# A two-layer RWKV-7 / GLA trunk on one core: `solve` takes its heads in turn, and the inversions, loads and scores of later blocks are placed earlier among the weight products

## The chip, the core and the metric

The kernel runs on one core of a Trainium2 chip. The metric is the device time in microseconds (us) of one execution, as the median over several runs. The engines: PE multiplies matrices (its weight loads are shown apart as PEld), DVE and ACT work on vectors, POOL here only fills memory, SP issues DMAs. Each engine takes its instructions in order.

## The reference

16 learned tokens are put ahead of 256, which makes T = 272 tokens of 2048 numbers. Two layers follow, each a token mixer and a squared-ReLU MLP (2048 to 8192 and back), with RMS norms before each and residual additions. The mixer of layer 1 is gated linear attention. The mixer of layer 0, where the change lies, is RWKV-7: 32 heads of 64, and for each head a 64x64 state that every token updates:

```python
sa = einsum('bhvk,bhk->bhv', S, a_t)
S = S * w_t[:, :, None, :] + sa[..., None] * b_t[:, :, None, :] + v_t[..., None] * k_t[:, :, None, :]
y = einsum('bhvk,bhk->bhv', S, r_t)
...
y = ((y - mu) * rsqrt(var + GN_EPS)) * ln_w + ln_b
out = ((y + bonus) * g) @ w_o
```

All is float32.

## The kernel before

**Weight products.** Activations lie with features on partitions and tokens along the free axis. A float32 product with a weight is made of three matmuls: each weight tile of 128x1024 is loaded (`raw`, L129), split by ACT into `hi` (L135) and by DVE into the rest `lo` (L136), and multiplied as hi by x, hi by the rest of x, lo by x (L141 to L143). `raw` has three buffers, `hi` and `lo` two each. Eight such triples use up one tile. I call a triple a unit; in the stage below `R(n)` writes n units, and `until(m)` as many as bring their number to m.

**The recurrence.** It runs in chunks of tokens, four of 64 and one of 16 (c = 0 to 4), for 16 heads at a time (g = 0, 1). A block is a pair of chunks of one g: block 0 holds chunks 0 and 1, block 1 chunks 2 to 4, blocks 2 and 3 the same for g = 1. For a block, `load(b)` fetches the keys and queries, written to memory before, into the tiles BK and AR (L419; two sets of tiles, for even and for odd blocks). `scores(c, e)` multiplies them for eight heads (L436, two PSUM banks `pt`), and DVE masks the result into AM (L269, "mask" below). `invert(b)` inverts the 64x64 triangles of all heads at once on DVE: transposes into `sysA` (L450, L455), 30 pairs of operations `upd`, `sysA` ("steps"), transposes back (L466 into a place that the merge reads, L470 into AM). It is a generator, and `some(inv, n)` emits n pieces of it. `merge(b)` (L557, L567, on PE) joins the halves of the triangles.

Per chunk, on PE: `state` (L629, L631: what the state S contributes), `solve` (L641: the inverse times the right side `rs`), `centre` (L580, of the next chunk), `carry` (L648: S itself), `learn` (L654: the new state in PSUM, which DVE scales into `sb`, shown as S), `inner` (L603, of the next chunk), `emit` (L663: the outputs), `keys` (L593: keys of the next chunk, transposed). `sides`, `centre`, `solve`, `emit` and `keys` are evicted by ACT. `uv` holds the values of the chunk in one half of the partitions and what `solve` gives in the other.

When a g is through, `norm(g)` takes four features' tiles at a time: a matmul (L681), two ACT operations, three of DVE (L687, L269, L693) and four matmuls with the gate (L692); `split` makes of the result the operands of the output product.

**What sets the order.** On PE the order is written out by hand in this stage (`manual_schedule`): the chunk steps, with units between them that cover their latencies. GAPS gives for each chunk the units before `solve` and after `carry`; MARK gives the number of units at which each of the four merges stands. For all other engines a scheduler chooses the order when the kernel is built; then it is fixed, and waits follow from it.

```python
                for h in range(q, 16, 2):
                    nc.tensor.matmul(pu[o : o + nu, h // 2], am[up, h, :nu], rs[up, h], start=True, stop=True)
                nc.scalar.copy(uv[n : n + nu, q::2], pu[o : o + nu])
```

Of the kernel before, what the change touches and what calls it, by code (L numbers as in the profile page):

```python
# [43 lines left out]

GAPS = [[(4, 4), (4, 4), (5, 4), (5, 4), (5, 5)],
        [(4, 4), (4, 4), (5, 4), (5, 4), (5, 5)]]

MARK = [120, 176, 244, 326]  # L50

OUTQ = [0, 1, 4, 5]
OUTA = [4, 5, 6, 7, 12, 13, 14, 15]
# [2 lines left out]
class Kern:  # L56
# [210 lines left out]
    def rwkv(self, done):  # L267
        nc, tc, ap = self.nc, self.tc, self.ap
# [329 lines left out]
        def inner(g, c):  # L598
            full, n, nr, am, lo, up, at = geom(c)
            uv = uvs[g, c]  # L600
            ra = ras[g, c] = bank(self.pu())
            for h in range(16):
                nc.tensor.matmul(ra[at[h % 2], h // 2], am[:n, h, :n], uv[:n, h], start=h < 2, stop=c == 0 and h > 13)  # L603
            if c == 0:
                sides(g, c)
# [28 lines left out]
        def solve(g, c):  # L634
            full, n, nr, am, lo, up, at = geom(c)
            uv, rs, pu = uvs[g, c], ras[g, c, "rs"], bank(self.pu())
            nu = n if full else 16
            for q in range(2):
                o = n * (1 - q)
                for h in range(q, 16, 2):  # L640
                    nc.tensor.matmul(pu[o : o + nu, h // 2], am[up, h, :nu], rs[up, h], start=True, stop=True)  # L641
                nc.scalar.copy(uv[n : n + nu, q::2], pu[o : o + nu])


# [22 lines left out]
        def norm(g):  # L667

            def square(f):
                sq = self.t(kp, [P, T], "ysq", 2)  # L670
                nc.scalar.activation(sq, hres[:, f], AF.Square)
                return sq

            nxt = square(4 * g)
            yield
            for f in range(4 * g, 4 * g + 4):
                sq = nxt
                g2 = self.t(kp, [P, 2, P], "g2", 2)
                nc.sync.dma_start(g2, ap["g2"][f])
                va = self.pry()[:, :T]  # L680
                nc.tensor.matmul(va, self.bones, sq, start=True, stop=True)  # L681
                nc.scalar.activation(sq, va, AF.Ln, scale=1.0 / HEAD, bias=self.eps[GN_EPS])
                nc.scalar.activation(sq, sq, AF.Exp, scale=-0.5)
                if f < 4 * g + 3:
                    nxt = square(f + 1)
                yield
                nc.vector.scalar_tensor_tensor(out=sq, in0=hres[:, f], scalar=self.vec("ln_w", f), in1=sq, op0=ALU.mult,  # L687
                                               op1=ALU.mult)
                tt(rr[f], rr[f], sq, ALU.add)
                pg = self.pm()[:, :T]  # L690
                for i in range(2):
                    nc.tensor.matmul(pg, g2[:, i], gs[i], start=i == 0, stop=i == 1)  # L692
                nc.vector.scalar_tensor_tensor(out=hres[:, f], in0=rr[f], scalar=self.vec("ln_b", f), in1=pg,  # L693
                                               op0=ALU.add, op1=ALU.mult)
                normed.add(f)
                yield
# [82 lines left out]
        def R(n):  # L779
            for _ in range(n):  # L780
                if next(work, work) is not work:
                    ran[0] += 1
# [4 lines left out]
        def some(it, n):  # L787
            for _ in range(n):
                next(it, None)

        nothing = iter(())
        self.split_parts = 2
        load(1)
        ahead()
        with tc.manual_schedule(engines={mybir.EngineType.PE}):
            R(10)
            for c, e in ((2, 0), (2, 1), (3, 0), (3, 1), (4, 0)):
                some(inv, 7)
                R(16)
                scores(c, e)  # L800
            for g in range(2):
                last, quarter = nothing, 0
                if g:

                    last = norm(0)
                    some(last, 1)
                    for _ in range(4):
                        R(3)
                        some(last, 2)
                    last = chain(last, norm(1))  # L810
                until(MARK[2 * g])
                some(inv, 99)
                m = merge(2 * g)
                next(m)
                some(last, 1)
                R(4)
                some(last, 1)
                next(m)
                some(last, 1)
                until(128 + 128 * g)  # L820
                centre(g, 0)
                some(last, 1)
                R(2)
                keys(g, 0)
                some(last, 1)
                R(2)
                inner(g, 0)
                some(last, 3)
                if g:

                    for c, e in ((2, 0), (2, 1), (3, 0), (3, 1), (4, 0)):
                        R(3)
                        scores(c, e)
                        some(last, 2)
                    assert next(last, None) is None
                else:
                    R(2)
                inv = invert(2 * g + 1)
                for c in range(5):
                    if c == 2:  # L840
                        until(MARK[2 * g + 1])
                        some(inv, 99)
                        m = merge(2 * g + 1)
                        next(m)
                        R(4)
                        next(m)
                        R(4)
                    if c:
                        state(g, c)
                    if g == 0 and c in (2, 3):  # L850
                        scores(c - 2, 0)
                    R(GAPS[g][c][0])
                    some(inv, 11)
                    solve(g, c)
                    if c < 4:
                        centre(g, c + 1)
                    if g == 0 and c in (2, 3):
                        scores(c - 2, 1)
                    if c < 4:
                        carry(g, c)  # L860
                    R(GAPS[g][c][1])
                    if g == 0 and c == 3:
                        inv = invert(2)
                    some(inv, 11)

                    if c < 4:
                        learn(g, c)
                        inner(g, c + 1)
                    emit(g, c)
                    if c < 3:  # L870
                        keys(g, c + 1)
                    if g == 0 and c == 1:
                        load(2)
                    if g == 0 and c == 4:
                        load(3)
            for g in (2, 3):
                for _ in norm(g):
                    R(g)
# [256 lines left out]
```

## Time and profile before

| | |
|---|---|
| median of three runs | 2623.42 us (2621.15 to 2627.11) |
| the profiled execution | 2624.24 us |
| its span, first to last instruction | 2622.0 us |
| PE busy | 2555.0 us, 97% |
| DVE busy | 1667.9 us, 64% |
| ACT busy | 1239.7 us, 47% |
| mean granted clock of PE | 0.987 |

The profile is of one execution. A row of a group reads: line, engine, operation, out<-in, size, count, then busy time and mean of one in ns, then the idle time of the engine just before such instructions and what ended it. A float32 matmul shows as two instructions, so eight heads are x16. In a table of stretches each row gives the stretch, its length, the busy time of PE, PEld, DVE, ACT and POOL with their counts, the clock that PE was granted (1.00 is full) and the share and rate of the DMA engines. A list of waits gives the waiting engine and line, who released it, the sum in us, how often, and the longest.

### The profile page before, as it was taken

What the parts mean: (1) busy time and instruction counts of PE and PEld (TensorE: products, weight loads), DVE (VectorE), ACT (ScalarE), POOL (GpSimd) and SP (SyncE); (2) the same over time, 40 slices, a digit from 0 to 9 for tenths busy, and PEclk for the clock granted to TensorE, in tenths of its full rate; (3) what the DMA queues carried; (4) which work ended last, traced back from release to release, by engine and by line L of the source; (5) the groups of instructions that cost most, each with busy time, mean ns of one, the idle gap of its engine ahead of it and who ended that gap; (6) DMA issues with size and microseconds to landing.
All of it is one profiled execution on the core that took longest, in us unless ns stands there. A gap on an engine that the chain in (4) does not pass through costs nothing.

```text
span 2622.0 us, 47088 instructions
## 1 busy us (share of the span) xinstructions
PE 2555.0 (97%) x19274; PEld 2364.8 (90%) x19274; DVE 1667.9 (64%) x2745; ACT 1239.7 (47%) x1941; POOL 9.3 (0%) x32
## 2 busy tenths in 40 slices
PE   9999799889999999999999999999999999999998
PEld 8898788788999999999999989998888888888887
DVE  8687985774755545545546676677766666656665
ACT  5376343434544434434434454455555535445344
POOL 0000000000000000000000000000000000000000
PEclk9999899889999999999999999999999999999999
DMA  5578543312455555555555544454555555555554
GB/s 201 175 239 276 195 138 98 115 67 86 164 175 176 177 177 177 177 176 175 175 176 176 178 151 149 145 173 153 185 189 189 187 191 186 190 188 187 191 185 160
DMA packets 140120, 450.13 MB, mean 172 GB/s; under 512 B 14704, under 2 KB 30832, under 8 KB 139904
## 3 DMA queue, kind: packets, MB, share of 16 engines
q1 hardware_dynamic: 139904, 447.12, 50.4%
q8 instruction: 151, 2.47, 0.4%
q14 instruction: 65, 0.53, 0.1%
HBM read 431.07 MB, written 15.99 MB: 171 GB/s over the span
## 4 chain that ended last, share of the span: by engine, by line
PE 78%; DVE 2%; ACT 1%; DMA 0%; issue 0%; DVEq 0%
PE pj L169 24%; PE pj L141 13%; PE pj L143 13%; PE pj L142 13%; PE pj L170 12%; DVE lo L136 1%; PE pt L970 1%; PE pu L641 0%; PE pu L979 0%; PE pm L692 0%; PE pt L959 0%; PE pu L981 0%; PE pry L681 0%; PE pm L580 0%; PE pm L916 0%; PE pu L980 0%
## 5 line engine op out<-in xcount | busy, mean ns | idle before, releaser
L135 ACT CAST hi<-raw 128x1024 fp32r<-128x1024 f32 (+2 forms) x838 | 814.0, 979 | 1121.4 <-PE pj L142 612.7
L136 DVE TENSOR_TENSOR lo<-raw,hi 128x1024 fp32r<-128x1024 f32 (+2 forms) x838 | 946.7, 1136 | 601.4 <-ACT hi L135 593.4
L141 PE MATMUL pj<-x,hi 128*128 128x272 f32 x2272 | 676.7, 298 | 6.1 <-DVE hres L269 4.1
L143 PE MATMUL pj<-x,lo 128*128 128x272 f32 x2272 | 661.0, 291 | 1.7 <-DVE lo L136 1.7
L142 PE MATMUL pj<-x,hi 128*128 128x272 f32 x2272 | 659.3, 290 | 0.0
L169 PE MATMUL pj<-x,hi 128*128 128x512 f32 x1664 | 585.8, 396 | 0.6 <-DVE x L889 0.6
L170 PE MATMUL pj<-x,lo 128*128 128x256 f32 x1664 | 466.7, 281 | 1.3 <-DVE lo L136 1.3
L141 PEld LDWEIGHTS pj<-x,hi 128*128 128x128 f32 x2272 | 431.9, 190 | 16.9 <-issue 6.1
L142 PEld LDWEIGHTS pj<-x,hi 128*128 128x128 f32 x2272 | 434.6, 191 | 4.2 <-issue 2.0
L143 PEld LDWEIGHTS pj<-x,lo 128*128 128x128 f32 x2272 | 431.6, 190 | 2.9 <-DVE lo L136 1.9
L169 PEld LDWEIGHTS pj<-x,hi 128*128 128x128 f32 x1664 | 312.5, 188 | 76.7 <-issue 2.9
L169 PE MATMUL pj<-h,hi 128*128 128x512 f32 x1024 | 358.5, 394 | 0.0
L170 PEld LDWEIGHTS pj<-x,lo 128*128 128x128 f32 x1664 | 313.3, 188 | 2.2 <-DVE lo L136 1.9
L141 PE MATMUL pj<-h,hi 128*128 128x272 f32 x1024 | 294.7, 288 | 0.0
L143 PE MATMUL pj<-h,lo 128*128 128x272 f32 x1024 | 293.9, 287 | 0.0
L142 PE MATMUL pj<-h,hi 128*128 128x272 f32 x1024 | 293.6, 287 | 0.0
L170 PE MATMUL pj<-h,lo 128*128 128x256 f32 x1024 | 288.5, 282 | 0.0
L169 PEld LDWEIGHTS pj<-h,hi 128*128 128x128 f32 x1024 | 192.4, 188 | 44.5
L142 PEld LDWEIGHTS pj<-h,hi 128*128 128x128 f32 x1024 | 193.7, 189 | 0.0
L170 PEld LDWEIGHTS pj<-h,lo 128*128 128x128 f32 x1024 | 193.5, 189 | 0.0
L141 PEld LDWEIGHTS pj<-h,hi 128*128 128x128 f32 x1024 | 192.6, 188 | 0.0
L143 PEld LDWEIGHTS pj<-h,lo 128*128 128x128 f32 x1024 | 192.1, 188 | 0.0
(247 smaller groups left out, 2095.4 us busy)
## 6 DMA issues: line engine op xcount, KB each, us to landing
raw<-mlp_w_d SPq DMA_DIRECT2D x512, 512.0 KB, 3.3
raw<-gla_in_d SPq DMA_DIRECT2D x98, 512.0 KB, 3.3
raw<-w_rkv_d SPq DMA_DIRECT2D x80, 512.0 KB, 3.5
raw<-gla_o_d SPq DMA_DIRECT2D x32, 512.0 KB, 3.3
raw<-rw_oQ_d SPq DMA_DIRECT2D x24, 512.0 KB, 3.3
raw<-w_r_d SPq DMA_DIRECT2D x16, 512.0 KB, 3.3
ard<-ar SPq DMA_DIRECT2D x16, 288.0 KB, 3.6
bkd<-bk SPq DMA_DIRECT2D x16, 288.0 KB, 4.0
```

What stands on the lines that cost most here:

```text
L135: nc.scalar.copy(hi[:, h], raw[:, h])
L136: nc.vector.tensor_tensor(out=lo[:, h], in0=raw[:, h], in1=hi[:, h].bitcast(F32), op=ALU.subtract)
L141: nc.tensor.matmul(out, hi[:, ws], xh, start=first, stop=False)
L142: nc.tensor.matmul(out, hi[:, ws], xl, start=False, stop=False)
L143: nc.tensor.matmul(out, lo[:, ws], xh, start=False, stop=last)
L169: nc.tensor.matmul(wide, hi[:, ws], x[kt][:, :, off : off + SEQ], start=kt == 0, stop=False)
L170: nc.tensor.matmul(ps[:, :SEQ], lo[:, ws], x[kt][:, 0, off : off + SEQ], start=False, stop=kt == nk - 1)
L970: nc.tensor.matmul(pa[:w, i * C : (i + 1) * C], KX[i][:, dt, s * P : s * P + w], Q[:, dt, i * C : (i + 1) * C], start=dt == 0, stop=dt == 1)
```

## The change

Nothing is computed in another way. `solve` issues its 16 heads in their order, which alternates between the two halves of the output's partitions, and both evictions come after the last. GAPS are smaller, and are the same for both g: 2 or 3 units after `carry` instead of 4, 4 before `solve` instead of 5 in chunks 2 and 3. Merges 1, 2 and 3 stand at fewer units. 26 units instead of 10 are written ahead of the first loop over block 1's scores, each of whose blocks has 16 more before it. For g = 1 the scores of block 3 move from behind merge 2 to between the pieces of `norm(0)`, and all of `norm(1)` behind merge 2. `invert(2g + 1)` is begun right behind merge 2g and spread over what follows; `invert(2)` begins one step sooner, as `scores(1,1)` does. The loads of blocks 2 and 3 are split in two, the keys first.

```diff
-GAPS = [[(4, 4), (4, 4), (5, 4), (5, 4), (5, 5)],
-        [(4, 4), (4, 4), (5, 4), (5, 4), (5, 5)]]
-MARK = [120, 176, 244, 326]
+GAPS = [(4, 2), (4, 2), (4, 2), (4, 3), (5, 5)]
+MARK = [120, 170, 240, 310]
...
+            for h in range(16):
+                o = n * (1 - h % 2)
+                nc.tensor.matmul(pu[o : o + nu, h // 2], am[up, h, :nu], rs[up, h], start=True, stop=True)
             for q in range(2):
                 o = n * (1 - q)
-                for h in range(q, 16, 2):
-                    nc.tensor.matmul(pu[o : o + nu, h // 2], am[up, h, :nu], rs[up, h], start=True, stop=True)
                 nc.scalar.copy(uv[n : n + nu, q::2], pu[o : o + nu])
...
+        units1 = ((2, 0), (2, 1), (3, 0), (3, 1), (4, 0))
...
-            R(10)
-            for c, e in ((2, 0), (2, 1), (3, 0), (3, 1), (4, 0)):
+            R(26)
+            for c, e in units1:
                 some(inv, 7)
                 R(16)
                 scores(c, e)
             for g in range(2):
-                last, quarter = nothing, 0
+                last = nothing
                 if g:
                     last = norm(0)
                     some(last, 1)
-                    for _ in range(4):
+                    for c, e in units1:
                         R(3)
                         some(last, 2)
-                    last = chain(last, norm(1))
+                        scores(c, e)
+                    last = norm(1)
                 until(MARK[2 * g])
                 some(inv, 99)
                 m = merge(2 * g)
                 next(m)
                 some(last, 1)
                 R(4)
-                some(last, 1)
                 next(m)
-                some(last, 1)
+                inv = invert(2 * g + 1)
+                some(inv, 4)
                 until(128 + 128 * g)
...
-                some(last, 3)
-                if g:
-                    for c, e in ((2, 0), (2, 1), (3, 0), (3, 1), (4, 0)):
-                        R(3)
-                        scores(c, e)
-                        some(last, 2)
-                    assert next(last, None) is None
-                else:
+                for _ in last:
                     R(2)
-                inv = invert(2 * g + 1)
+                    some(inv, 2)
+                R(2)
                 for c in range(5):
...
                     if g == 0 and c in (2, 3):
-                        scores(c - 2, 0)
-                    R(GAPS[g][c][0])
-                    some(inv, 11)
+                        scores(c - 2, c - 2)
+                        if c == 3:
+                            inv = invert(2)
+                    R(GAPS[c][0])
+                    some(inv, 9)
                     solve(g, c)
                     if c < 4:
                         centre(g, c + 1)
-                    if g == 0 and c in (2, 3):
-                        scores(c - 2, 1)
+                    if g == 0 and c == 2:
+                        scores(0, 1)
                     if c < 4:
                         carry(g, c)
-                    R(GAPS[g][c][1])
-                    if g == 0 and c == 3:
-                        inv = invert(2)
-                    some(inv, 11)
+                    R(GAPS[c][1])
+                    some(inv, 9)
                     if c < 4:
                         learn(g, c)
                         inner(g, c + 1)
+                    if g == 0 and c == 2:
+                        scores(1, 0)
                     emit(g, c)
                     if c < 3:
                         keys(g, c + 1)
-                    if g == 0 and c == 1:
-                        load(2)
-                    if g == 0 and c == 4:
-                        load(3)
+                    if g == 0:
+                        if c == 0:
+                            fetch(2, BKs, bkd)
+                        if c == 1:
+                            fetch(2, ARs, ard)
+                        if c == 2:
+                            fetch(3, BKs, bkd)
+                        if c == 4:
+                            fetch(3, ARs, ard)
+                    some(inv, 7)
```

How this moves instructions on engines whose order the scheduler makes. SP, at the load of block 1, before (`raw` are weights; BK and AR the block's tiles; `g` the gate's weights) and, in the second list, after:

```order
L129 DMA raw_3716<-w_rkv_d 128x1024
L419 DMA BK_618_3436<-bkd_79 128x8x320
L129 DMA raw_3751<-w_rkv_d 128x1024
L419 DMA AR_619_3437<-ard_80 128x8x320
L679 DMA g_877_5521<-g_d 128x256
```

```order
L128 DMA raw_3683<-w_rkv_d 128x1024
L418 DMA BK_618_3436<-bkd_79 128x8x320
L128 DMA raw_3718<-w_rkv_d 128x1024
L128 DMA raw_3783<-w_rkv_d 128x1024
L418 DMA AR_619_3437<-ard_80 128x8x320
L128 DMA raw_3818<-w_rkv_d 128x1024
```

One more weight stands between BK and AR.

DVE in `norm(0)`, between S of chunk 3 and the end of inversion 2, before and after (`upd` and `sysA` are steps of the inversion, `AM<-pt` masks of block 3):

```order
L687 SCALAR_TENSOR_TENSOR ysq_5510<-hres_72,vecs_121,ysq_5510 128x272
L269 TENSOR_TENSOR sysA_1934<-sysA_1934,upd_5410 64x17x14
L269 TENSOR_TENSOR r_7_81<-r_7_81,ysq_5510 128x272
L136 TENSOR_TENSOR lo_5564<-raw_5561,hi_5563 128x512 x2
L269 TENSOR_TENSOR upd_5458<-sysA_1934 64x240
L693 SCALAR_TENSOR_TENSOR hres_72<-r_7_81,vecs_121,pm_5531 128x272
L269 TENSOR_TENSOR sysA_1934<-sysA_1934,upd_5458 64x16x15
L687 SCALAR_TENSOR_TENSOR ysq_5527<-hres_72,vecs_121,ysq_5527 128x272
```

```order
L687 SCALAR_TENSOR_TENSOR ysq_5485<-hres_72,vecs_121,ysq_5485 128x272
L268 TENSOR_TENSOR upd_5317<-sysA_1934 64x238
L268 TENSOR_TENSOR r_7_81<-r_7_81,ysq_5485 128x272
L268 TENSOR_TENSOR sysA_1934<-sysA_1934,upd_5317 64x14x17
L693 SCALAR_TENSOR_TENSOR hres_72<-r_7_81,vecs_121,pm_5514 128x272
L268 TENSOR_TENSOR upd_5382<-sysA_1934 64x234
L268 TENSOR_TENSOR AM_620_3438<-pt_5518,cst_120 128x4x128
L268 TENSOR_TENSOR sysA_1934<-sysA_1934,upd_5382 64x13x18
L268 TENSOR_TENSOR AM_620_3438<-pt_5519,cst_120 128x4x128
L268 TENSOR_TENSOR upd_5385<-sysA_1934 64x228
L687 SCALAR_TENSOR_TENSOR ysq_5510<-hres_72,vecs_121,ysq_5510 128x272
```

Two masks now stand between one tile's norm and the next. From S of chunk 3 to the last transpose of inversion 2 DVE's queue holds, before, 60 steps, 6 transposes back, 5 `lo`, 4 norms, 7 additions and 4 transposes into the merge's place; after, 48 steps, the same transposes, 5 `lo`, 4 norms, 10 masks, 2 additions and 4 first transposes of inversion 3. From there to S of chunk 0 of g = 1 it holds, after, 44 steps of inversion 3, 12 transposes, 7 `lo`, 4 norms, 8 splits and 9 additions.

DVE again, around that S of g = 1, before and after. In `upd` the last number is the row's size; the steps begin with 30 and grow to 240 and shrink again:

```order
L269 TENSOR_TENSOR upd_6210<-sysA_1934 128x108
L269 TENSOR_TENSOR r_8_82<-pj_6088,r_8_82 128x272
L269 TENSOR_TENSOR sysA_1934<-sysA_1934,upd_6210 128x27x4
L136 TENSOR_TENSOR lo_6341<-raw_6338,hi_6340 128x512 x2
L269 TENSOR_TENSOR upd_6213<-sysA_1934 128x130
L269 TENSOR_TENSOR sysA_1934<-sysA_1934,upd_6213 128x26x5
L269 TENSOR_TENSOR S_3440<-pu_6187,WC_97 128x512
```

```order
L268 TENSOR_TENSOR upd_6249<-sysA_1934 128x210
L268 TENSOR_TENSOR sysA_1934<-sysA_1934,upd_6249 128x10x21
L268 TENSOR_TENSOR r_8_82<-pj_6138,r_8_82 128x272
L268 TENSOR_TENSOR upd_6252<-sysA_1934 128x198
L135 TENSOR_TENSOR lo_6396<-raw_6393,hi_6395 128x512 x2
L268 TENSOR_TENSOR sysA_1934<-sysA_1934,upd_6252 128x9x22
L268 TENSOR_TENSOR S_3440<-pu_6226,WC_97 128x512
```

S stood behind the tenth step of inversion 3, and stands now behind its 44th.

## The prediction

> **What bounds the kernel now.** I read the page first, then the list of PE's waits, then busy time stretch by stretch, and last the timelines at the places that the change touches. The page:
>
> ```profile
> span 2622.0 us, 47088 instructions
> ...
> PE 2555.0 (97%) x19274; PEld 2364.8 (90%) x19274; DVE 1667.9 (64%) x2745; ACT 1239.7 (47%) x1941; POOL 9.3 (0%) x32
> ```
>
> PE carries the kernel. The change only redistributes matmuls, apart from what runs inside `solve`, so a gain must come from PE time that is lost. The waits of PE from 285 to 700 us, where the edited stage lies (line, releaser, sum, times, longest):
>
> ```profile
> PE pt L436 <- DMA AR<-ard: 12.6, 1, 12.6
> PE pt L557 <- DVE sysA L466: 11.0, 2, 8.2
> PE pu L641 <- ACT uv L642: 6.7, 10, 0.7
> ```
>
> One load (L419 into AR), two late inversions (merge, L557), ten waits in the middle of `solve` (L641). Busy time by stretch; the columns that matter are length, PE, DVE and PEclk:
>
> ```profile
> 299.46:312.06 12.60, 0.02 (x1) 0.03 (x1) 11.73 (x29) 0.32 (x1) 0.00 (x0) 0.70 0.88 294
> 312.06:318.15 6.09, 6.09 (x34) 5.87 (x35) 5.66 (x15) 0.00 (x0) 0.00 (x0) 0.50 0.01 3
> 431.28:492.71 61.43, 46.95 (x485) 41.84 (x483) 45.76 (x115) 21.02 (x45) 0.15 (x1) 0.86 0.38 121
> 448.85:492.71 43.86, 32.13 (x278) 29.25 (x278) 36.80 (x100) 16.04 (x36) 0.00 (x0) 0.84 0.41 128
> 492.71:540.24 47.53, 44.85 (x573) 39.07 (x574) 32.15 (x69) 21.54 (x45) 1.11 (x2) 0.93 0.27 85
> 540.24:574.56 34.32, 29.20 (x349) 26.06 (x349) 32.86 (x82) 11.61 (x21) 0.00 (x0) 0.94 0.24 87
> 574.56:623.37 48.81, 46.80 (x792) 41.62 (x793) 10.73 (x19) 20.20 (x38) 0.95 (x1) 0.86 0.13 45
> ```
>
> I call these stretches by what stands at their ends: the load's stall; the half clock behind it; C, from the end of `state(0,3)` to merge 2, whose second part begins when S of chunk 3 is written; D1, from merge 2 to `state(1,1)`; D2, on to merge 3; E, on to the end of `emit(1,4)`. In C and D2 DVE is as full as PE: there the inversion's chain on DVE ends last. A lost us also drops the clock: the six us behind the load's stall run at 0.50.
>
> **The change part by part.**
>
> *solve.* A solve, what follows it, and an `inner` of the same shape, from PE's timeline (start, length):
>
> ```profile
> 530.37 1.14 PE L641 MATMUL pu<-rs,AM 64*64 64x64 f32 x16
> 532.18 1.14 PE L641 MATMUL pu<-rs,AM 64*64 64x64 f32 x16 [0.67 <-ACT uv L642]
> 533.25 1.09 PE L580 MATMUL pm<-cst,hres 128*64 128x128 f32 x16
> ...
> 535.98 1.15 PE L654 MATMUL pu<-uv,bkt 128*64 128x64 f32 x32
> 537.06 1.15 PE L603 MATMUL pu<-uv,AM 64*64 64x64 f32 x32
> ```
>
> And a block of scores with the first matmuls of a unit behind it (a unit is three matmuls of a weight product, for one tile of the contraction):
>
> ```profile
> 524.41 1.16 PE L436 MATMUL pt<-AR,BK 64*128 64x128 f32 x16
> 525.50 0.39 PE L141 MATMUL pj<-x,hi 128*128 128x272 f32 x1
> 525.73 0.29 PE L142 MATMUL pj<-x,hi 128*128 128x272 f32 x1
> 525.86 0.29 PE L143 MATMUL pj<-x,lo 128*128 128x272 f32 x1
> ```
>
> Scores take 525.50 - 524.41 = 1.1 us; a matmul 525.86 - 525.73 = 0.13, a unit 0.38, and the first after a change of shape 0.10 more (0.39 in length against 0.29).
>
> Eight heads of one parity write one half of the partitions and take 1.1 us; then PE waits for the eviction, and the other eight take 1.1 more: 533.25 - 530.37 = 2.88 us. `inner` (L603) sends its 16 heads to the two halves in turn, as `solve` now will; twice the matmuls take 1.15, the length of one pass of `solve`, and 1.08 from start to start (537.06 - 535.98, of the like `learn` above it). So each of ten solves shrinks by 1.8 us (I take the chunk of 16 tokens as equal). What goes behind are two evictions on ACT:
>
> ```profile
> L642 ACT COPY uv<-pu 64x512 f32<-64x512 f32 (+1 forms) x20 | 11.6, 579 | 37.7 <-PE pu L641 37.7
> ```
>
> Two of them end 0.1 + 2 x 0.58 = 1.3 us after the last matmul. Before `learn` reads them PE now has `centre` (1.0 us of its 1.09), the carry where there is one, and two units instead of four: 1.8 us at the least. So the smaller fill costs nothing, unless a weight cast lands on ACT in between. Nearest bounds: nothing, or ten times a missing 0.5 us, 5 us; I take nothing, since in the new order of ACT the casts stand ahead of or behind the pair. The Trainium skill (TensorEngine Tiling, PSUM Bottleneck) warns that packing speeds up the matmuls but not the copies out of PSUM, which may then bind. By that rule the upper end holds and the sum below is 5 us less; the trace's cover of 1.8 us against 1.3 decides for the lower, and no run yet shows the pair behind.
>
> *The first load.* SP issues in order; these are its issues before the stall, and the landing of the two block loads:
>
> ```profile
> 298.87 0.37 SPq L419 DMA_DIRECT2D BK<-bkd  x1
> 301.87 0.33 SPq L129 DMA_DIRECT2D raw<-w_rkv_d  x1
> 302.30 0.38 SPq L419 DMA_DIRECT2D AR<-ard  x1
> ```
>
> ```profile
> BK<-bkd SPq DMA_DIRECT2D x1, 1280.0 KB, 7.7
> AR<-ard SPq DMA_DIRECT2D x1, 1280.0 KB, 9.6
> ```
>
> PE stands from 299.46 to 312.06. Sixteen more units (6.0 us) now run before the first `scores`; their weights are loaded ahead, three buffers deep. But the new order of SP puts one more weight load ahead of AR, and that one waits for a `lo` on DVE which cannot be written before PE has finished six of the sixteen units (about 302), the cast and DVE's queue: about 305. AR then is issued near 305 instead of 302.3, behind half a MB more. Much of the delay hides, since BK and the earlier weight fill the queue until about 306 (1.8 MB at the 294 GB/s of the stall's row are 6.2 us); what is left is the 0.5 MB, about 1 to 2 us. So the first term is -6.0 + 1.0 = **-5 us** (between -3.5 and -8, the latter if the half clock behind the stall shrinks too). The load can't go away: 42 units end near 305.5, AR lands near 313.
>
> *Earlier inversions, norm among scores.* This is decided by DVE's in-order queue, so I count it there. Mean times in the second part of C (the first fence) and from 285 to 700 us (the second):
>
> ```profile
> L269 DVE TENSOR_TENSOR upd<-sysA 64x30 f32<-64x30 f32 (+14 forms) x30 | 9.6, 321 | 0.6
> L269 DVE TENSOR_TENSOR sysA<-sysA,upd 64x30 f32<-64x30 f32 (+14 forms) x30 | 9.6, 321 | 0.7
> L136 DVE TENSOR_TENSOR lo<-raw,hi 128x512 fp32r<-128x512 f32 x10 | 6.4, 681 | 1.8 <-ACT hi L135 1.8
> L470 DVE STREAM_TRANSPOSE AM<-sysA 32x256 f32<-32x256 f32 x7 | 4.3, 618 | 0.2
> L687 DVE SCALAR_TENSOR_TENSOR ysq<-hres,vecs,ysq 128x272 f32<-128x272 f32 x4 | 2.0, 490 | 3.7 <-ACT ysq L683 3.7
> L693 DVE SCALAR_TENSOR_TENSOR hres<-r,vecs,pm 128x272 f32<-128x272 f32 x4 | 1.9, 483 | 0.0
> L269 DVE TENSOR_TENSOR r<-r,ysq 128x272 f32<-128x272 f32 x4 | 1.7, 427 | 0.0
> ```
>
> ```profile
> L269 DVE TENSOR_TENSOR AM<-pt,cst 128x512 f32<-128x512 f32 x24 | 15.4, 684 | 19.5 <-PE pt L436 19.5
> L269 DVE TENSOR_TENSOR S<-pu,WC 128x512 f32<-128x512 f32 x8 | 5.5, 686 | 8.5 <-PE pu L654 8.4
> ```
>
> The first seven rows are 35.5 us; with four more transposes (2.5) and seven more additions of 0.43 us (3.0) the queue holds 41.0 us of work in a stretch of 43.86: a factor of 1.07 for what DVE idles.
>
> Up to S of chunk 3, after: `scores(1,1)` now comes right behind `state(0,3)` and ends 1.1 us after it; two masks 1.4, eight transposes 4.9, the ones on POOL 0.3 (9.3 / 32), twelve small steps 3.2 (the shortest rows; my estimate is a sixth of the 19.2 us of all 60), S 0.7: 11.6 us, where it took 448.85 - 431.28 = 17.6. From S to the end of inversion 2, after: 48 steps 16.0, 6 + 4 + 4 transposes 8.7, ten halves of `lo` 6.4, four norms 5.6, ten masks 6.8, additions 0.9: 44.4, times 1.07 = 47.5 us, where it took 43.86. So the inversion starts sooner, but the masks of the next block and the first transposes of inversion 3 now stand in its way: merge 2 comes at 59.1 instead of 61.43. PE's own work there (46.95 us before) is no longer than that, so its slack is spent waiting, at the masks and at `norm` instead of at merge 2.
>
> D1, after: from the end of inversion 2 DVE has to pass 44 steps 15.1 (19.2 less the last sixteen, short ones too, at 0.26), 6 + 6 transposes 7.4, fourteen halves of `lo` 9.0, four norms 5.6, eight splits 3.4, nine additions 3.9, S 0.7: 45.1, times 1.07 = 48.3 us, before S of chunk 0 is out and `state(1,1)` may start. PE's work there falls (44.85 before; five blocks of scores, 5.4 us, and a solve's 1.1 us leave it, one unit comes), to about 39. So S is a new wait, of some 10 us, where `state(1,1)` had none: D1 48.3 against 47.53. D2, after: 30 units instead of 43 (the mark is 310 instead of 326, and the fills are smaller), 4.9 us; one solve, 1.8; and merge 3 no longer waits (11.0 - 8.2 = 2.8), since after S only 16 short steps and 6 transposes are left of inversion 3, some 9 us, while PE has 20 us to go: 34.32 - 9.5 = 24.8. C to D2 together: 59.1 + 48.3 + 24.8 = 132.2 against 143.3, -11.1. Of these, 7 units (2.6) are only done later, and one block of scores (1.1) is done earlier: **-7.4 us** net.
>
> *The rest.* Three solves before C: **-5.4**. E: three solves, -5.4, and its clock. Two windows at half clock, the first in the middle of small matmuls, the second at merge 3:
>
> ```profile
> 437.61:441.02 3.41, 3.41 (x33) 2.58 (x27) 0.00 (x0) 1.56 (x3) 0.00 (x0) 0.50 0.02 5
> 574.14:584.38 10.24, 9.82 (x156) 9.22 (x160) 3.06 (x6) 4.06 (x10) 0.00 (x0) 0.50 0.16 55
> ```
>
> If 24 units run unbroken into merge 3, the 10.24 us need not be at half: between 0 and 5 us (half of 10.24). The window at 437.61 is at 0.50 with no gap near it but a solve's 0.67 us, so small matmuls alone may keep one, and I take 3: E **-8.4**. The Trainium skill (TensorE: Matmul & The Clock Gate, Why this matters for your kernels) advises only against PE gaps over about 3 us; by it all 5 us would come back, and the sum would be 2 us lower. This case's trace disagrees. The loads for blocks 2 and 3 are issued sooner; AR's 9.6 us to landing and C's 61 show that they can come in time, and I put them at nothing (bounds: 0, or some 2 us if the weights in front of them on SP are late). The 21 units taken out of the fills run at the end, as work that is only moved.
>
> Sum: -5.0 - 5.4 - 7.4 - 8.4 = -26.2. The profiled execution took 2624.24 us (span 2622.0), 0.8 over the median 2623.42: 2624.2 - 26.2 = 2598.0, and less the 0.8, **2597 us**.
>
> **The rivals.** (1) DVE keeps pace: if the queue has no idle time (factor 1.00: 44.4 and 45.1 instead of 47.5 and 48.3, -6 us) and the first term is -8 instead of -5, the time is 2588; if PE moreover keeps its clock throughout E (-2) and the splits and additions ahead of S in D1 (7.3 us) fall into times when DVE would wait, 2580. For it: the new order fills DVE's waits for ACT (3.7 us at L687) with steps. Against: S in D1 is behind 44 steps whatever PE does. (2) The evictions bind and `lo` is late in the fills before the merges: 5 us for the evictions, 0.4 us for each of some 14 weights in C and D1, 2608. For it: `lo` stands behind steps in the new queue. (3) It does not do what it says: alternate parities share the rows of their operands and do not overlap, so `solve` only loses its 0.67 us: -7 instead of -18 on PE, six solves outside C and D1 lose 1.1 us less each, 2604. Against: `inner` has the same rows and overlaps. (4) Slower: DVE and PE in lockstep. A mask waits for scores, scores for the bank that the last mask empties, `norm` for `hres`, and DVE's queue is in order, so what one waits the other can't use. If each of five mask pairs cost a turn of PE (three units, a norm, a block of scores, 3.6 us plus 1 on ACT) and each of eight norms the 0.9 us of L687 (3.7 / 4), DVE idles 23 + 7 = 30 us: 2627. It decides against the change from 26 us of idle on; the steps between the masks, 2 us a turn, speak against it.
>
> **How the numbers follow.** Forecast 0.62, rival 1 0.14, rival 2 0.10, rival 3 0.04, rival 4 0.06, anything else 0.04. The range goes from rival 1's 2580 to just past rival 2, 2611. A difference under 0.2% (5 us) can't be told from none here: faster 0.91 (the first four cases), same 0.04, slower 0.05 (rival 4's upper half and others).
>
> **What would show it.** `solve`: one group of 32 in 1.08 us, no wait on L642 in PE's list, perhaps some at `learn`. The load: AR issued near 305, PE's wait 7 to 8 us. Inversions: no wait, or under 2 us, at either merge, and instead waits of PE for S (L631) near 10 us, for masks and for `hres` of L693. Half clock at 574 to 584 gone. The prediction is wrong if PE's wait for S is small (DVE faster than counted), or if waits for masks exceed some 15 us in all.

## The result, and the profile after

The changed kernel takes 2582.67 us in the median of four runs (2580.29 to 2583.18), the kernel before 2625.27 beside it. The ratio is 0.9838, with a 95% interval from 0.9821 to 0.9855: 42.6 us less, where 26.2 were forecast. In several kernels below some executions took about 10 us more than the others at the same granted clock; where a median holds such runs I go by the stretches of the profiled execution. The one of the changed kernel took 2583.18 us, and 2580.9 of span. Its page:

```profile
span 2580.9 us, 47093 instructions
...
PE 2530.7 (98%) x19274; PEld 2342.7 (91%) x19274; DVE 1667.4 (65%) x2745; ACT 1240.7 (48%) x1941; POOL 9.3 (0%) x32
```

PE is busy for 24.3 us less (it was 2555.0) and idle for 16.8 us less (67.0 became 50.2). The same matmuls run, so the first of these is passes of `solve` that now overlap, and clock. Line numbers after are one less than before. PE's waits from 285 to 700 us:

```profile
PE pt L435 <- DMA AR<-ard: 8.0, 1, 8.0
PE pm L692 <- DVE hres L693: 6.4, 6, 2.7
PE pj L142 <- DVE lo L135: 3.6, 4, 1.5
...
PE pt L435 <- DVE AM L268: 1.6, 3, 0.9
...
PE pu L630 <- DVE S L268: 0.7, 1, 0.7
```

The waits at the merges (11.0 us) and in `solve` (6.7) are gone. The stretches, with the columns of the prediction's fence (length; PE, PEld, DVE, ACT, POOL; clock; DMA): from the last product of the keys' loop to the first `scores`, on to merge 0, B (merge 0 to the end of `state(0,3)`), C, D1, D2, E, and the tail up to the end of the stage:

```profile
293.67:315.23 21.56, 13.53 (x105) 13.27 (x105) 20.62 (x55) 6.37 (x13) 0.00 (x0) 0.89 0.90 310
315.23:355.40 40.17, 38.69 (x331) 36.88 (x331) 37.46 (x78) 11.71 (x24) 0.00 (x0) 0.93 0.31 108
355.40:419.89 64.49, 63.08 (x1206) 57.15 (x1205) 46.37 (x106) 35.44 (x70) 2.06 (x3) 1.00 0.36 117
419.89:473.85 53.96, 47.94 (x581) 41.30 (x579) 51.08 (x123) 19.99 (x42) 0.15 (x1) 1.00 0.36 117
473.85:515.05 41.20, 35.15 (x481) 30.96 (x481) 40.00 (x100) 24.01 (x52) 1.11 (x2) 1.00 0.44 139
515.05:535.44 20.39, 20.39 (x309) 18.96 (x308) 16.48 (x38) 9.27 (x17) 0.00 (x0) 1.00 0.19 67
535.44:571.32 35.88, 35.88 (x778) 32.12 (x778) 8.79 (x16) 19.05 (x36) 0.94 (x1) 1.00 0.21 71
571.32:655.66 84.34, 81.29 (x593) 77.43 (x589) 68.58 (x143) 50.50 (x108) 0.00 (x0) 1.00 0.43 145
```

The clock column is 1.00 from merge 0 to the end of the stage, where C, D1, D2 and E had 0.86, 0.93, 0.94 and 0.86. DVE is now busy for 95% of C and 97% of D1. To compare the stretches one has to take out work that only changed its place. I counted units and blocks of scores in both traces, and price a unit at 0.38 us and a block at 1.1:

| stretch | before | after | units, scores | net | forecast |
|---|---|---|---|---|---|
| to merge 0 | 68.1 | 61.7 | 0, 0 | -6.4 | -5.0 |
| B | 71.2 | 64.5 | -9, +1 | -4.4 | -5.4 |
| C, D1, D2 | 143.3 | 115.6 | -7, -1 | -24.0 | -7.4 |
| E | 48.8 | 35.9 | -5, 0 | -11.0 | -8.4 |
| tail | 75.3 | 84.3 | +21, 0 | +1.0 | 0 |

These are -44.8 us. Outside the stage the profiled execution lost 3.7 us (1.7 ahead, where a window at half clock lies at 252 us, and 2.0 behind), which makes the spans' difference of 41.1. What goes beyond the forecast lies in C to D2: 16.6 us, of which 5.1 are in C (53.96 us where 59.1 were forecast), 7.1 in D1 (41.20, not 48.3) and 4.4 in D2 (20.39, not 24.8).

### The profile page after: what moved, and what is told of

Same layout as the page of the kernel before. It is cut to its first block, busy times and chain, and to the rows that moved or that the text cites. A ratio compares the mean times of both kernels' runs of the same rounds, so it can differ in the third digit from the quotient of the medians.

```text
span 2580.9 us, 47093 instructions
## 1 busy us (share of the span) xinstructions
PE 2530.7 (98%) x19274; PEld 2342.7 (91%) x19274; DVE 1667.4 (65%) x2745; ACT 1240.7 (48%) x1941; POOL 9.3 (0%) x32
## 4 chain that ended last, share of the span: by engine, by line
PE 91%; DVE 6%; ACT 1%; DMA 1%; issue 1%; DVEq 0%; POOL 0%; SPq 0%; ACTq 0%; POOLq 0%
PE pj L168 24%; PE pj L140 15%; PE pj L142 15%; PE pj L141 15%; PE pj L169 12%; DVE lo L135 2%; PE pj L195 1%; DVE upd L268 1%; DVE sysA L268 1%; PE pt L973 1%; DMA ca<-cad 0%; ACT hi L134 0%; PE pu L982 0%; DVE AM L469 0%; PE pry L141 0%
## 5 line engine op out<-in xcount | busy, mean ns | idle before, releaser
L140 PEld LDWEIGHTS pj<-x,hi 128*128 128x128 f32 x2272 | 428.3, 189 | 15.5 <-issue 4.6
```

The costliest lines, as they stand in the source:

```text
L140: nc.tensor.matmul(out, hi[:, ws], xh, start=first, stop=False)
```

## Experiments

**Solve alone.** The kernel before with the new `solve`.

```diff
+for h in range(16):
+    o = n * (1 - h % 2)
+    nc.tensor.matmul(pu[o : o + nu, h // 2], am[up, h, :nu], rs[up, h], ...)
 for q in range(2):
     o = n * (1 - q)
-    for h in range(q, 16, 2):
-        nc.tensor.matmul(pu[o : o + nu, h // 2], am[up, h, :nu], rs[up, h], ...)
     nc.scalar.copy(uv[n : n + nu, q::2], pu[o : o + nu])
```

> The kernel before with nothing but the new solve. Theory A (the solve is worth 1.8 us only where PE sets the pace): three solves ahead of C and three in E give -5.4 each, the one in D1 -1.8, and the three in C and D2 nothing, since there the inversion on DVE ends last and the waits at merges 2 and 3 grow by what the solves lose: -12.6, about 2612. Theory B (the clock): the ten waits inside solve are also what holds the granted clock at half in C to E; without them the windows at 0.50 between 437 and 595 us mostly go, and the gain is -20 or more. Theory C (no stage matters): -18. Theory D (the two evictions at the end bind): -8 or less, with waits of PE at learn.

Measured: 2610.04 us, ratio 0.9934 (0.9914 to 0.9955). Its stretches C, D2 and E:

```profile
427.99:482.24 54.25, 40.46 (x483) 36.22 (x484) 45.88 (x115) 21.04 (x45) 0.15 (x1) 0.93 0.44 138
528.36:565.03 36.67, 27.52 (x347) 25.41 (x348) 34.51 (x87) 11.21 (x20) 0.00 (x0) 0.94 0.26 87
565.03:605.22 40.19, 40.19 (x793) 36.29 (x793) 10.79 (x19) 20.18 (x38) 0.94 (x1) 0.93 0.18 55
```

Theory A is right on D2, which grew by 2.4 us, as merge 3 waits longer, and wrong on C, which lost 7.2 us: its clock went from 0.86 to 0.93, while PE idled there as before (13.8 us against 14.5). That a slow PE had held back the inversion fits this, but is argued, not shown. E lost 8.6 us, 5.4 by passes and the rest by clock (0.86 to 0.93). So A's stages and B's clock both act, and the 15.5 us between the medians lie between them. C's 18 us lie within the interval too, but C has neither the longer D2 nor the clock. D (the evictions bind) is out: no wait at `learn` stands in its list.

**The old solve in the changed kernel.** The same edit the other way.

> The changed kernel with the old solve put back (two passes of eight heads, an eviction behind each). Theory A: seven solves lie where PE sets the pace, +12.6; three (chunks 3 and 4 of g = 0, chunk 0 of g = 1) lie in C and D1, where DVE was busy for 97% of the time after the change, and cost nothing: about 2595. Theory B (the clock): beside that, windows at half clock come back in C to E, 3.4 us each and several of them, which makes +18 to +25, about 2601 to 2608. Theory C: +18 with no change of clock.

Measured: 2599.62 us, ratio to before 0.9897 (0.9876 to 0.9917): 17 us more than with the new one by the medians, 15 by the ratios. C ran 3.6 us longer (57.56), D1 stayed (41.34), E took 5.5 more (41.34) with no window at half clock, but in B three came back. The clock changes only at borders 3.41 us apart; I call what lies between two of them a cell. The first window, with the cell ahead of it, and the timeline of the solve in that cell:

```profile
367.08:370.49 3.41, 2.74 (x41) 2.39 (x41) 3.27 (x8) 1.38 (x4) 0.00 (x0) 1.00 0.14 24
370.49:373.91 3.42, 3.42 (x28) 2.84 (x26) 3.06 (x7) 1.51 (x3) 0.00 (x0) 0.50 0.35 134
```

```profile
367.27 1.14 PE L640 MATMUL pu<-rs,AM 64*64 64x64 f32 x16
369.08 1.14 PE L640 MATMUL pu<-rs,AM 64*64 64x64 f32 x16 [0.67 <-ACT uv L641]
```

0.67 us of idle in a cell of 3.41 us, and the next cell is granted half. B became 9.3 us longer, 5.4 of it three solves. A window in C besides (6.83 us) stands behind a wait of 3.2 us for a mask. Theory B has the mechanism, windows that come back, but its size is just missed (+17, of +18 to +25) and its place is not right: they came in B and C, not in E. C's +18 is near in size, but it had no change of clock.

**The load alone.** The kernel before with `R(26)` for `R(10)`.

> The kernel before with 26 units instead of 10 ahead of the loop over block 1's scores, and nothing else. My theory: PE's wait for AR falls from 12.6 to about 8 us and the half clock behind it from 13.65 to 10.24 us, merge 0 comes 5 to 6.5 us sooner, and as no wait of the stage behind it depends on block 1, the whole of it stays: -5 to -6.5, about 2618. Rival: merges 2 and 3 wait for the inversion on DVE anyway and take it back: 0 to -2.

Measured: 2622.67 us, ratio 0.999 (0.9972 to 1.0008). Merge 0 stood 6.4 us nearer, as expected (61.73 us behind the same point, as in the changed kernel). But the stage as a whole became only 2.9 us shorter, near the rival's 0 to -2, and by another way than its own; the interval alone would not exclude either. This is C, which had 61.43 us, 46.95 of PE and a clock of 0.86:

```profile
425.21:488.82 63.61, 49.16 (x483) 43.89 (x483) 45.77 (x115) 20.93 (x45) 0.15 (x1) 0.79 0.37 117
```

PE idles as long as before (63.61 - 49.16 = 14.45 us, against 14.48); it is busy 2.2 us longer, at a lower clock, and D1 lost 2.1 in the same way. In the changed kernel nothing from merge 0 on falls to half clock, and there the 6.4 us stay.

**Block 1's load in four pieces**, in the changed kernel.

```diff
-load(1)
+for k in range(2):
+    for dst, src in ((BKs, bkd), (ARs, ard)):
+        nc.sync.dma_start(dst[1][:, 4 * k : 4 * k + 4],
+                          src[4 * k : 4 * k + 4, :, 256:576].rearrange("f p n -> p f n"))
```

> The changed kernel with block 1's load in four pieces: the keys and queries of the first eight heads, then of the other eight (each 640 KB). Theory of bytes: the stall is the time of 2.56 MB and the weights between them at 310 GB/s. The first scores need only the first two pieces and one weight between them, 1.8 MB, 6 us from the first issue near 301: PE's wait for AR falls from 8.0 to 0 to 2 us, the half clock behind it goes or shrinks, -7 to -11, about 2574. Rival (the issue): weight loads that wait for their buffer stand between the pieces on SP, the second pieces are issued near 310, and the second scores wait instead: 0 to -3.

Measured: 2581.16 us, ratio to before 0.9838 (0.9813 to 0.9864). PE's wait:

```profile
PE pt L435 <- DMA AR<-ard: 3.5, 1, 3.5
```

It fell from 8.0 to 3.5 us, not to under 2, and merge 0 came 2.9 us sooner (58.86 against 61.73). Most of that is not fewer bytes, but the place in SP's queue, where one weight instead of two now stands between the keys and the queries:

```profile
300.80 0.33 SPq L128 DMA_DIRECT2D raw<-w_rkv_d  x1
301.23 0.37 SPq L796 DMA_DIRECT2D AR<-ard  x1
304.50 0.33 SPq L128 DMA_DIRECT2D raw<-w_rkv_d  x1
```

Counted from the start of the first stretch, the first piece of AR is issued 9.7 us in, and AR was at 13.4: 3.7 us sooner. It took 7.2 us to land, hardly less than the 8.0 of the whole, though it has half the bytes. The theory of bytes had 6 us from the first issue to the landing, and it took 9.9. The time, 1.5 us below the changed kernel's, does not tell the two apart: the size is the rival's, though no second `scores` waits for a load.

**Block 3's scores behind merge 2**, in the changed kernel, and inversion 3 begun behind them.

```diff
 for c, e in units1:
     R(3)
     some(last, 2)
-    scores(c, e)
 last = norm(1)
...
-inv = invert(2 * g + 1)
-some(inv, 4)
...
 for _ in last:
     R(2)
-    some(inv, 2)
+if g:
+    for c, e in units1:
+        R(3)
+        scores(c, e)
 R(2)
+inv = invert(2 * g + 1)
```

> The changed kernel with block 3's scores put back behind merge 2 (three units ahead of each), and inversion 3 begun behind them; all else as changed. Theory (DVE's queue decides, in rows that take 0.9 of their summed lengths): C loses ten masks and some transposes on DVE and five blocks of scores on PE and ends near 46 us instead of 53.9; D1 gains five blocks and fifteen units, 46 instead of 41.2; in D2 49 steps of inversion 3 stand behind S of chunk 0 instead of 16, merge 3 waits some 10 us and the clock behind it drops, 28 instead of 20.4. In all +4 to +10, about 2587 to 2593. Rival: where the scores stand does not matter, the same masks and steps pass DVE in any case: 0, about 2583. Second rival: it is the source of nearly all that C to D2 gained: +15 or more.

Measured: 2599.89 us, ratio to before 0.9895 (0.9868 to 0.9921), 17 us more than the changed kernel by the medians, 15 by the ratios. The wait at the merges, and the 10 us of E behind merge 3:

```profile
PE pt L556 <- DVE sysA L465: 11.3, 2, 9.3
```

```profile
549.09:558.94 9.85, 9.85 (x156) 9.22 (x160) 3.08 (x6) 4.06 (x10) 0.00 (x0) 0.50 0.16 57
```

The first theory is right on C, which is 47.15 (it said 46), on D2, 27.07 (28), and on merge 3, which waits 9.3 us (10). It is wrong on D1, 54.41 us where it said 46: there 6.8 us lie at half clock, which costs 3.4, and PE idles for 4.6, of which the theory had nothing. The sum is the second rival's, since the clock that the waits cost is larger than the theory had it: C has 0.96, D1 0.94, D2 0.80 and E 0.88, all of which had 1.00. E alone is 4.2 us longer (40.04) with the same matmuls. The run takes back two things at once, the place of the scores and the sooner start of inversion 3, and does not tell them apart.

**The old fills and marks** in the changed kernel (GAPS and MARK of the kernel before).

> The changed kernel with the fills and marks of before (4 and 4, 4 and 4, 5 and 4, 5 and 4 units; merges at 120, 176, 244, 326). Theory of the prediction: units are only moved, from the end of the stage into C to E, and the two evictions behind solve are covered by either fill: within 3 us of the changed kernel, 2580 to 2586, with E and D2 longer by their units at 0.38 us and the tail shorter by the same. Rival 1: in C and D1 DVE sets the pace, so units put there are free and shorten the tail: -3 to -5. Rival 2: the smaller fills bring the inversions and merges together: +5.

Measured: 2582.88 us, ratio to before 0.9823 (0.9799 to 0.9846). No difference, as the prediction had it: B to E took 13.6 us more and the tail 9.1 less. C and D1 (0.91 and 0.88) hold three windows at half clock, of 6.83, 3.41 and 10.24 us, which the smaller fills did not have; that the 4.5 us between the two sums are theirs is argued.

**Does DVE set the pace in C and D1?** Three kernels. First, two kinds of its work given to POOL:

```diff
-tt(yo[f][:, 1], hres[:, f], yo[f][:, 0].bitcast(F32), ALU.subtract)
+nc.gpsimd.tensor_tensor(out=yo[f][:, 1], in0=hres[:, f], in1=yo[f][:, 0].bitcast(F32), op=ALU.subtract)
...
-tt(rr[f], rr[f], hres[:, f])
+nc.gpsimd.tensor_tensor(out=rr[f], in0=rr[f], in1=hres[:, f], op=ALU.mult)
```

> The changed kernel with two kinds of DVE's work given to POOL: the subtraction in split (eight in D1, 3.4 us) and the product of r with hres behind a weight product (some five in C and D1, 2.1 us). Theory (DVE, 97% busy in C and D1, sets the pace there): C shorter by about 1.3, D1 by about 4 us, PE's waits for hres of the gate's product and for lo shrink: -4 to -6, about 2577 to 2579. Rival 1: PE's own order sets the pace, DVE is only full beside it: 0. Rival 2, the Trainium skill (SBUF - State Buffer, on the port pair that DVE and GpSimd share): a DVE operation with two SBUF inputs and a POOL operation lock each other out, so nothing is won and each of DVE's steps that meets a POOL operation waits for it, 0 to +5.

Measured: 2585.18 us, ratio to before 0.9832 (0.9808 to 0.9856), the same time. D1 rose from 41.20 to 42.89. Groups of POOL and DVE in its D1, and the same two of DVE in the D1 of the changed kernel:

```profile
L705 POOL TENSOR_TENSOR x<-hres,x 128x272 fp32r<-128x272 f32 x8 | 8.6, 1074 | 19.9 <-ACT x L704 19.7
...
L268 DVE TENSOR_TENSOR upd<-sysA 128x168 f32<-128x168 f32 (+14 forms) x24 | 9.7, 404 | 0.5
...
L268 DVE TENSOR_TENSOR sysA<-sysA,upd 128x184 f32<-128x184 f32 (+14 forms) x23 | 9.4, 408 | 0.6
```

```profile
L268 DVE TENSOR_TENSOR sysA<-sysA,upd 128x184 f32<-128x184 f32 (+14 forms) x23 | 8.0, 348 | 0.5
L268 DVE TENSOR_TENSOR upd<-sysA 128x184 f32<-128x184 f32 (+14 forms) x23 | 8.0, 348 | 0.4
```

Ten operations of 0.43 us left DVE in D1 (4.3 us), and its steps took 404 to 408 ns instead of 348 (+3.1 us), besides a longer `lo` and `ysq`. DVE was busy for 41.27 us instead of 40.00. The Trainium skill (SBUF - State Buffer, SBUF: two separate sides) says that a DVE operation with two inputs in SBUF and a POOL operation that reads SBUF shut each other out; the trace agrees, in that what left DVE came back as longer steps. Rival 2's 0 to +5 holds the 2.5 us between the medians; rival 1's 0 is not excluded by this run, but is by the next ones. Together with the split load:

> The load of block 1 in four pieces and POOL's share together, as the best candidate. If both work and are independent: -4 for the load as its own run gave, and -4 to -6 more, about 2573 to 2575. If POOL's share does nothing: 2578, as the split load alone.

Measured: 2583.8 us, ratio to before 0.9819 (0.9796 to 0.9843), neither 2573 to 2575 nor 2578, and not told from the changed kernel. POOL's share does nothing for it either. This is its D1:

```profile
473.92:516.81 42.89, 35.41 (x481) 31.00 (x481) 41.27 (x92) 24.07 (x52) 11.12 (x12) 1.00 0.41 131
```

With POOL's share alone D1 had a window at half clock (0.96) and PE was busy for 36.74 us; here it has none, and PE is busy for 35.41. DVE's busy time and D1's length are the same in both, to 0.01 us.

So the work has to go, not to move. The second kernel leaves some of it out, and with it the bonus term of the outputs:

```diff
-tt(rr[f], rr[f], hres[:, f])
...
-tt(rr[f], rr[f], sq, ALU.add)
...
-nc.vector.scalar_tensor_tensor(out=hres[:, f], in0=rr[f], scalar=self.vec("ln_b", f), ...)
+nc.vector.scalar_tensor_tensor(out=hres[:, f], in0=sq, scalar=self.vec("ln_b", f), ...)
```

> The changed kernel without two of DVE's operations: the product of r with hres behind a weight product, and norm's addition of ysq to r (the gate's product then takes ysq alone), so the bonus term is left out of what is computed. DVE passes 13 rows of 0.43 us less in C and D1, 0.35 us each from start to start. Theory (DVE sets the pace in C and D1): C and D1 together 95.1 - 4.6 = 90.5 us, in all -4 to -5, about 2578. Rival (PE's order sets the pace): C and D1 together stay within 1 us of 95.1.

Measured: 2586.92 us, ratio to before 0.9869 (0.985 to 0.9888), a median of four runs from 2579.71 to 2594.7; the profiled execution is that of 2579.71. Its C and D1:

```profile
423.43:475.47 52.04, 47.43 (x578) 41.23 (x579) 49.02 (x116) 19.89 (x42) 0.15 (x1) 1.00 0.34 111
475.47:513.58 38.11, 35.12 (x481) 31.03 (x480) 36.91 (x92) 23.71 (x52) 1.11 (x2) 1.00 0.41 129
```

52.04 + 38.11 = 90.15 us against 95.16, with the same PE work in both: the 90.5 of the theory. In C and D1 DVE sets the pace. The whole time does not show it: the median is 4 us above the changed kernel's. The third kernel adds work:

```diff
 tt(rr[f], rr[f], sq, ALU.add)
+tt(sq, sq, sq)
+tt(sq, sq, sq)
```

> The changed kernel with two more DVE operations per tile in norm (ysq squared in place twice, behind its last use; nothing reads it). Sixteen rows more, of which twelve to sixteen in C and D1. Theory (DVE sets the pace): C and D1 together 95.1 + 4.2 to 5.6 us, in all +4 to +6, about 2588. Rival (PE's order): under 1 us more.

Measured: 2597.18 us, ratio to before 0.9903 (0.9887 to 0.9919).

```profile
419.48:484.84 65.36, 53.94 (x578) 46.72 (x579) 57.91 (x138) 19.89 (x42) 0.15 (x1) 0.87 0.30 98
484.84:528.58 43.74, 38.95 (x481) 34.73 (x480) 37.98 (x98) 24.37 (x52) 1.12 (x2) 0.88 0.42 135
```

14 us more, not 4 to 6. C and D1 took 109.1 instead of 95.2 us. PE idled there for 16.2 instead of 12.1 us, 4.1 more where the theory had 4.2 to 5.6, and its busy time rose from 83.1 to 92.9 us for the same matmuls, at 0.87 and 0.88. So the theory holds, and its size leaves out the clock. That the longer waits let the clock fall, and that a slower PE is late for DVE in turn, is argued.

**More units where PE waits**: the split load, with five instead of three units ahead of each of block 3's scores, four instead of two between the pieces of `norm(1)`, and marks 250 and 332.

> The split load of block 1 and 22 units more in C and D1 (five instead of three ahead of each of block 3's scores, four instead of two between the pieces of norm(1); merges 2 and 3 at 250 and 332 units), taken from the end of the stage. PE idles for 12 us in C and D1 together, waiting for DVE. Theory (DVE sets the pace): the units cost PE there only what their 2.75 weights cost DVE, 5.5 halves of lo, 3.5 us, and save 22 x 0.38 = 8.4 us at the end: -5 against the split load alone, about 2574. Rival: the units stand where PE does not wait, or the additions and lo behind them push DVE as far back as PE gained: 0, about 2579; with a half clock saved or lost either way.

Measured: 2576.35 us, ratio to before 0.9821 (0.9807 to 0.9835), the lowest median of all, but not one that is told from the changed kernel's 0.9838. D1 fell to 36.18, and C rose to 62.69, since the built order puts two of block 3's masks behind the end of inversion 2 and PE waits 8.1 us for masks. By the stretches it is the rival: C and D1 take 98.9 us against 95.0 with the split load alone, D2 4.5 more, and the tail 9.4 less.

## Why the prediction was right in sign and short in size

**Solve: right.** One group of 32 in the timeline of the changed kernel, and nothing waits for the evictions:

```profile
379.71 1.15 PE L639 MATMUL pu<-rs,AM 64*64 64x64 f32 x32
380.79 1.09 PE L579 MATMUL pm<-cst,hres 128*64 128x128 f32 x16
...
383.63 1.15 PE L654 MATMUL pu<-uv,bkt 128*64 128x64 f32 x32
```

380.79 - 379.71 = 1.08 us, as `inner`. So rival 3 is out, and of rival 2 the evictions; its late `lo` is there in small (PE waits 3.6 us for it instead of 1.7). The lower end that the cover of 1.8 us gave for the evictions was the right one. What was missing is the clock that the ten waits cost besides.

**The load: right.** The order of SP did what was said:

```profile
300.81 0.37 SPq L418 DMA_DIRECT2D BK<-bkd  x1
302.94 4.04 SPq L128 DMA_DIRECT2D raw<-w_rkv_d  x2
307.08 0.38 SPq L418 DMA_DIRECT2D AR<-ard  x1
```

All this stands 1.7 us later in this execution, so AR went out at 305.4 in the prediction's time (near 305), and PE waited 8.0 us (7 to 8). The half clock behind it shrank too, from 13.65 to 10.24 us, one of the bounds: -6.4 instead of -5.

**C to D2: the step that failed is "a factor of 1.07 for what DVE idles".** The counts were right. From S of chunk 3 to the end of inversion 2 I had 44.4 us of rows, and the trace holds 96 rows of 45.3 us; up to S of chunk 0, 45.1, and the trace 100 rows of 45.8. But they took 41.35 and 41.9 us, 0.91 of their sum, instead of 47.5 and 48.3. A row's length is not what it costs the queue; DVE's timeline shows why:

```profile
444.19 0.39 DVE L268 TENSOR_TENSOR upd<-sysA 64x238 f32<-64x238 f32 x1
444.51 0.43 DVE L268 TENSOR_TENSOR r<-r,ysq 128x272 f32<-128x272 f32 x1
444.86 0.39 DVE L268 TENSOR_TENSOR sysA<-sysA,upd 64x238 f32<-64x238 f32 x1
445.18 0.48 DVE L693 SCALAR_TENSOR_TENSOR hres<-r,vecs,pm 128x272 f32<-128x272 f32 x1
```

The second starts 0.32 us behind the first, which is 0.39 long: where an instruction does not need the one before it, they overlap by 0.07 to 0.08 us. In the second part of C before, 99 rows of 41.1 us were 36.8 us of busy time, with 7.1 of idle beside it: my 1.07 was 0.90 for the overlap times 1.19 for the idle. I carried the idle over, and the new order took it away (40.27 us busy of the 41.35). So S of chunk 0 was out when PE came, and the wait of 10 us at `state(1,1)` does not exist, which was the sign named for "DVE faster than counted". Rival 1's condition (no idle in the queue) came true, and more than its factor of 1.00. The time, too, is rival 1's (2580 to 2588) and not the forecast's 2597, though rival 1 had only 0.14; its lower end, 2588 less 2 and 7.3, is 2578.7 and not 2580, which changes nothing here.

**The clock: mis-sized.** The same time can be told from PE's side. In C, D1 and D2 I gave it nothing, since DVE bound them, and in E 3 us. Before, PE was busy at half clock for 23.4 us in C to D2 and for 13.2 in E (added over the windows at 0.50), which is 11.7 and 6.6 us lost; after, for none. With 10.2 us less of idle (22.3 to 12.1) and four second passes (4.3), C to D2 come to 26.2 us, against the -24.0 of the table. D2's part of the miss is of this kind: PE was its limit after the change, and the forecast had left it 1.7 us of clock (a window of 3.41 us at half) and 1.7 of waits. For E, 5.4 + 6.6 = 12.0 stand against -11.0. The prediction doubted that E's clock would all come back, because a window at 437.61 had only a solve's 0.67 us near it. The doubt was the wrong way round: that window was the solve's doing (with the new solve alone none stands there), and the change takes the solve's wait out. The Trainium skill's rule on gaps over about 3 us, cited there, gave the better sum for E. The old solve's trace disagrees with its size of a gap, since 0.67 us were followed by half clock in B.

**The rest.** No wait for AR or BK shows in g = 1, so the sooner loads cost nothing, as assumed; what they give was not tried by itself, nor was beginning the inversions sooner without the scores. The moved units cost what was said, within 1 us.

## What to carry to other kernels

Before a queue is forecast from summed row lengths, compare that sum with the engine's busy time in the same stretch, and keep overlap and idle apart: the first stays, the second is what a new order changes. Where the profile shows a clock under 1.00, price a short wait in the midst of small matmuls by the window behind it too, here 3.4 us at half speed (1.7 us lost) behind 0.67 us of waiting. A wait taken away alone may give less than its length: the load's 6.4 us came to 2.9 over the stage, because windows behind it grew. An engine that is full in one stretch was helped here by less work, and not by giving part of it to POOL.

## What the hardware showed that was not expected

The granted clock changes on a grid of 3.41 us. Over the 13 traces of this case, and the cells of that grid that lie between 285 and 720 us, all 30 cells at full clock in which PE was busy for less than 0.43 of the time were followed by a cell at half, and none of the 1197 at full clock that were at least 0.95 busy. Between these it depends: of 27 cells with a wait in the old `solve` and no other, busy for 0.73 to 0.80, nine were followed by half clock and 18 were not; with the new `solve` no cell busier than 0.64 was. Among the 27 the place on the grid tells most of it: eight held both passes of a solve whole, to within 0.01 us, and seven of these were followed by half clock; of the other 19, in which a border cut the solve, two were. So whether the same wait costs a window goes largely by where it falls on the grid, and a shift of a few us ahead of it can change that; it would explain why the windows moved from run to run, but no run here shifts the work on purpose. Why one of the eight was not followed and two of the 19 were stays open. This is a count over traces, made afterwards, and the two solve runs are the only ones that take such a wait away or put it back by itself.

An operation of 0.43 us on DVE takes 0.78 to 1.07 us on POOL here (the means in D1), and with ten of them in D1 the mean of DVE's steps there is 16% longer.
